# Three data movements of a hybrid decoder layer: gate stores moved to SyncE, a spilled operand loaded behind the value weights, raw value weights asked for earlier

## The chip, the cores and the metric

The kernel runs on one core of a Trainium2 chip. The metric is the device time of one execution in microseconds, the median of three runs. Five engines work side by side: TensorE (PE), VectorE (DVE), ScalarE (ACT), GpSimd (POOL) and SyncE (SP). ScalarE, GpSimd and SyncE also issue DMAs, each from its own instruction queue. An engine takes its instructions in order, so a DMA issue that has to wait for its data holds up everything behind it on that engine.

## The reference

One layer of a decoder trunk for a prompt of 2048 tokens and 8 single-token samples, 1024 wide, all in float32:

```
hn = rmsnorm(x, g_norm) * (1 + scale) + shift          # scale, shift, gate from silu(c) @ w_ada
z  = hn @ w_in                                          # xa, za (1024 each), q, k (512), v (1024), glr (16), zg (1024)
# RG-LRU: causal conv4 of xa, two block-diagonal gates, real-gated linear recurrence h, times silu(za)
# GLA, 4 heads (key 128, value 256): S_t = diag(alpha_t) S_{t-1} + k_t^T v_t, o_t = q_t S_t,
#   alpha from glr @ w_gla_g2; o = rmsnorm(o) * g_gla_norm * silu(zg)
x  = x + gate * (concat(y_lru, y_gla) @ w_out)
y  = rmsnorm(x, g_final)
```

The outputs are y for prompt and samples and the new convolution, recurrence and GLA states.

## The kernel before, in words

A float32 operand is split into a high part that TensorE multiplies in one pass and a low part, and a product is the sum of three passes: high times high, high times low, low times high. The three lines 661 to 663 (keys, queries, gates), 346 to 348 (values) and the loop of line 1566 are such triples.

The tokens are worked in two halves of 1024. `hn` of the half at work stands transposed in SBUF as `hh` (high) and `hl` (low), eight tiles of 128 features, 1024 columns and the samples. In each half the GLA heads follow in the order 3, 0, 1, 2 (`HEADS`), and between them stand the RG-LRU tiles. `gla_head` computes a head's values (`values`), then keys, queries and decay, and leaves the chunks of the recurrence to a list of due times (`after`, `tick`), so that they lie between later matrix products. In the second half, `values` also multiplies the samples by the raw, unsplit value weights (`sample_values`, line 912), which `raw_values` loads from `w_in` into the two buffers of the tag `wr` (line 333). Split weights lie in DRAM (`parts`) and are loaded by SyncE into the three buffers of the tag `w` (line 293).

Between the halves, `gates_ahead` computes gates of head 3 for the second tokens: six pieces of `silu2` (lines 1131 and 1132) that are stored in DRAM (`zgd`, line 1654) until the head's output needs them. In the same stretch `next_hn` modulates the next half of `hn`: TensorE transposes (line 197), ScalarE applies scale and shift (lines 199, 201), GpSimd rounds into `hh` (line 204) and VectorE forms `hl` (line 205). Behind it, seven-product schemes (`seven`, `product`, line 1566) compute further gates and RG-LRU inputs from sums of blocks of `hn`. One of these sums is put into the place of a block of `hn` itself, columns 512 to 1023 of the first four feature tiles (`a21`). That block is first spilled to DRAM (`a21d`, line 1524) and loaded back by `a21_back` (line 1532) for the values of head 3 in the second half, which read it from the fifth of their eight token tiles on.

Each engine's instruction order is settled when the program is compiled, by a scheduler with its own estimate of times: an instruction is placed when its inputs and its buffer are free in that estimate, in the order of the program where several are. Three helpers bend this order: `in_order` keeps the written order on each engine, `behind(q)` keeps what is written inside it behind the last instruction written for engine q, and `held(q)` makes the DMAs inside it wait until that last instruction has run.

Of the kernel before, what the change touches and what calls it, by code (L numbers as in the profile page):

```python
# [8 lines left out]
F32 = mybir.dt.float32  # L9
# [45 lines left out]
def hybrid_kernel(ctx, tc, i, o):  # L55
    nc = tc.nc
    V, S, G, PE, SP = nc.vector, nc.scalar, nc.gpsimd, nc.tensor, nc.sync
# [5 lines left out]
    def acc():  # L63
        return psum.tile([P, 512], F32, tag="acc", name="acc", bufs=4)
# [12 lines left out]
    zgd = dpool.tile([8, P, TH + NS], F32, tag="zgd", name="zgd")  # L77
    a21d = dpool.tile([2, P, 4, 512], F32, tag="a21d", name="a21d")
# [245 lines left out]
    def value_weights(h):  # L324
        n = DV + (RANK if h == HEADS[0] else 0)
        return [weights(V0 + h * DV, n, k0, 4) for k0 in (0, 4)]
# [12 lines left out]
    def drip():  # L339
        if drips:  # L340
            drips.pop(0)()
# [339 lines left out]
    def behind(q):  # L681

        return tc.issue_after(next(x for x in reversed(list(nc.cur_bb.bb.instructions)) if x.engine == q.engine))


    @contextmanager
    def held(q):

        traced = nc.cur_bb.bb.instructions
        mark = next(x for x in reversed(list(traced)) if x.engine == q.engine)  # L690
        before = {id(x) for x in traced}
        yield
        for x in list(traced):
            if id(x) not in before and x.engine in (SP.engine, G.engine):
                tc.add_manual_dep(x, mark.name, mybir.DependencyInfo(
                    mybir.DependencyClass.Sync, mybir.DependencyReason.DATA), reason="held")
# [4 lines left out]
    def after(units, fn, gla=False, val=False):  # L701
        clock[1] += 1
        heapq.heappush(pend, (clock[0] + units, clock[1], fn, gla, val))
# [221 lines left out]
    def new_values():  # L925
        while any(e[4] for e in pend):
            e = min(e for e in pend if e[3])
            pend.remove(e)
            heapq.heapify(pend)
            e[2]()  # L930
        return [[gp.tile([P, 4, DV], F32R, tag=tag, name=tag, bufs=2) for _ in range(2)] for tag in ("vh", "vl")]

    def values(half, h, w, back=None):
        first = h == HEADS[0]
        n = DV + (RANK if first else 0)
        vh, vl = new_values()
        turns = []
        for tt in range(8):
            if tt == 1 and back:
                with held(V):  # L940
                    back()
            if tt == 3 and half == 1:
                with held(V):
                    raw = raw_values(h, n)
            if tt == 4:
                while drips:
                    drip()
            if half == 0 or tt < 6:
                ps = acc()
                value_mm(ps[:, :n], slice(tt * P, (tt + 1) * P), w, n, (0, KT))  # L950
            elif tt == 6:
                both = [acc(), acc()]
                for k in (0, 4):
                    for m in range(2):
                        value_mm(both[m][:, :n], slice((6 + m) * P, (7 + m) * P), w, n, (k, k + 4))
                ps = both[0]
            else:
                ps = both[1]
            hi, lo = vh[tt // 4][:, tt % 4], vl[tt // 4][:, tt % 4]
            S.copy(hi, ps[:, :DV])  # L960
            V.tensor_tensor(lo, ps[:, :DV], hi.bitcast(F32), op=OP.subtract)  # L961
            if len(turns) == 3 or tt == 7 and turns:
                turns.pop(0)()
            if first:
                turns.append(low_rank(ps[:, DV:n], slice(0, P), tt * P))
            tick(0.5)
        if half == 1:
            turns.append(sample_values(h, raw, n))
        for f in turns:
            after(1, f, True)  # L970
        return vh, vl
# [201 lines left out]
    def gla_head(half, h, wv=None, ahead=None):  # L1173
        ns = len(SEGS[half])
        if wv:
            wk, wq = wkq0
            v, prep0, rest = first_head()
        else:
            w, back = value_weights(h), None
            if half and h == HEADS[0]:  # L1180
                back = a21_back
            v = values(half, h, w, back)
            wk = weights(K0 + h * DK, DK)
            wq = weights(Q0 + h * DK, DK)
        prep, zs, os_, state = {}, {}, [None], []

        def chunks(s, c):

            nch = min(SEGS[half][s][1], TH - SEGS[half][s][0]) // P
            if c == 0:  # L1190
                prep[s, "run"] = gla_start(half, h, s, prep[s])
                after(PACE[half][0], lambda: chunks(s, 1), True, True)
                return
            if c == nch and half:
                gate_load(s)
            gla_chunk(half, h, s, c - 1, prep[s], prep[s, "run"], v)
            if c < nch:
                after(PACE[half][1], lambda: chunks(s, c + 1), True, True)
                return
            gla_norm(nch, prep[s, "run"])  # L1200
            after(PACE[half][2] if half else 1 if s + 1 < ns else 2, lambda: finish(s), True)
            if s + 1 < ns:
                after(0, lambda: chunks(s + 1, 0), True, True)
            elif half == 1:
                G.dma_start(o[4][0, 0, h], St[h])

        def gate_load(s):
            c0, n = SEGS[half][s]
            for dt in range(2):
                z = new_zs()  # L1210
                G.dma_start(z[:, :n], zgd[2 * h + dt][:, c0:c0 + n])
                zs[s, dt] = z[:, :n]

        def finish(s):
            if (s, 1) not in zs or (s == 2 and os_[0] is None):
                after(0.5, lambda: finish(s), True)
                return
            gla_out(half, h, s, prep[s, "run"][1], os_[0] if s == 2 else None, [zs[s, 0], zs[s, 1]])

        def sample(smp, b0):  # L1220
            sample_state(h, smp, b0, state, lambda: os_.__setitem__(0, state[1]))

        pk = None
        if not wv:
            if h == HEADS[0]:

                pk = project(wk, *SEGS[half][0])
            dec = gla_decay(half, h, 0)
        for s in range(ns):
            if wv and s == 0:  # L1230
                prep[s] = prep0
                pk = project(wk, 512, 512)
                rest()
            else:
                prep[s] = gla_qk(half, h, s, wq, wk, dec, pk)
                pk = None
                if s == 0 and ahead:
                    with held(V):
                        ahead()
            if s + 1 < ns:  # L1240
                dec = gla_decay(half, h, s + 1)
            if s == 0:
                after(2 if h == HEADS[0] else 1, lambda: chunks(0, 0), True, True)
            tick()
        if half == 1:
            after(1, lambda: sample(prep[2][3], 0), True)
            after(3, lambda: sample(prep[2][3], 4), True)
        if wv:
            modulate_samples(st, xsr)
            hn_sample()  # L1250
            with tc.issue_after(last[V.engine]), tc.issue_after(last[S.engine]):
                constants()
            open_lp()
        if half == 1:
            return
        wz = [weights(ZG + (2 * h + dt) * P, P) for dt in range(2)]
        for s in range(ns):
            for dt in range(2):
                zs[s, dt] = gate_silu(wz[dt], s, 2 * h + dt)
                tick()  # L1260
# [225 lines left out]
    def a21():  # L1486
        return [(hh, hl)[u][:, :4, 512:TH] for u in range(2)]
# [39 lines left out]
        for n, u in ((0, 0), (1, 0), (0, 1), (1, 1), (2, 0), (2, 1), (3, 0), (3, 1), (4, 0), (4, 1)):  # L1527
            drips.append(lambda n=n, u=u: step(n, u))

    def a21_back():  # L1530
        for u, x in enumerate(a21()):
            G.dma_start(x.bitcast(F32), a21d[u])

    operands, lone, zq, zturn = [], [True], [], [0]

    def operand(src, shifted):
# [111 lines left out]
    def gates_ahead(h):  # L1648

        w = [weights(ZG + (2 * h + dt) * P, P) for dt in range(2)]  # L1650
        for c0, n in ((0, 256), (256, 256), (512, 512)):
            for dt in range(2):
                z = silu2(w[dt], c0, n)
                after(0.5, lambda z=z, dt=dt, c0=c0, n=n: S.dma_start(zgd[2 * h + dt][:, c0:c0 + n], z))
                tick(n / 512)
            if c0 == 256:
                while drips:
                    drip()
        sums()
# [521 lines left out]
    for n in range(2, 16):  # L2181
        g = n - 1
        x, prev = pairs[n], pairs[n - 1]
# [81 lines left out]
```

## Time and profile before

| | |
|---|---|
| Median of three runs | 1474.25 us (1472.72 to 1477.07) |
| Profiled execution | 1477.21 us, of which its span 1475.4 us |
| TensorE busy | 1435.1 us (97%) |
| VectorE, ScalarE, GpSimd busy | 1052.0, 688.7, 220.5 us |
| Mean granted TensorE clock | 0.988 |
| DMA traffic | 305.33 MB, 207 GB/s over the span |
| Spilled block of hn | two loads of 1024 KB from GpSimd, 6.7 and 8.3 us to landing |
| Raw value weights | eight loads of 512 to 544 KB from GpSimd, 4.8 to 8.1 us to landing |
| Gates stored by ScalarE in `gates_ahead` | four of 128 KB, two of 256 KB |

How to read the rows below: a row of a timeline has its start, its duration, the engine, the line of the kernel, the operation, what it writes and reads, and in brackets the engine's idle time just before it with what ended that. A row of waits has the total, the number and the longest. A row of a stretch has its bounds and length, then busy time and count for TensorE, its weight loads, VectorE, ScalarE and GpSimd, then the mean granted TensorE clock, the busy share of the DMA engines and GB/s. "SPq" and "ACTq" are instructions that only the engine's sequencer handles, such as DMA issues. Matmuls are pipelined, so a row of 0.29 us may follow another after 0.13 us.

### The profile page before, as it was taken

How to read it: one execution, taken by the hardware profiler on the slowest of the kernel's cores; microseconds unless marked ns; L12 is line 12 of the kernel's file. 1: busy time of each engine (PE TensorE's matmuls, PEld its weight loads, DVE VectorE, ACT ScalarE, POOL GpSimd, SP SyncE). 2: the span in 40 equal slices, each digit the busy share in tenths (PEclk: the TensorE clock that was granted, in tenths of full speed). 3: DMA queues.
4: the chain of work that ended last, by engine and by line, in shares of the span. 5: the costliest groups of instructions: out<-in, count | busy, mean ns of one | idle time of the engine just before them, and what ended most of it. 6: DMA issues, size and time to landing. Idle time of an engine off the chain costs nothing. (4 is left out here: it accounts for less than half of the span.)

```text
span 1475.4 us, 23576 instructions
## 1 busy us (share of the span) xinstructions
PE 1435.1 (97%) x8741; PEld 1262.3 (86%) x8741; DVE 1052.0 (71%) x2477; ACT 688.7 (47%) x1251; POOL 220.5 (15%) x366
## 2 busy tenths in 40 slices
PE   8999999999999999999999899998999999999998
PEld 6888989889898988788899899998998887778886
DVE  5757667776665769844468578585778986588886
ACT  4653544652544467534354354534557622144342
POOL 0200111222121112000212322323200000000000
PEclk9999999999999999999999999999999999999999
DMA  9655876866566454767646565656553757793453
GB/s 329 257 182 179 273 241 218 255 206 197 182 203 208 148 202 150 236 206 249 247 130 203 175 207 178 213 190 226 186 193 99 286 190 263 260 357 117 143 175 114
DMA packets 161241, 305.33 MB, mean 207 GB/s; under 512 B 12963, under 2 KB 91459, under 8 KB 158686
## 3 DMA queue, kind: packets, MB, share of 16 engines
q1 hardware_dynamic: 104917, 214.24, 42.6%
q0 software_dynamic: 23296, 72.54, 14.4%
q10 hardware_dynamic: 32912, 17.04, 3.8%
q8 instruction: 69, 1.13, 0.3%
q14 instruction: 47, 0.38, 0.1%
HBM read 188.51 MB, written 115.33 MB: 206 GB/s over the span
## 5 line engine op out<-in xcount | busy, mean ns | idle before, releaser
L661 PE MATMUL acc<-hh,w 128*128 128x512 f32 (+3 forms) x1112 | 388.8, 350 | 0.3 <-ACT tx L1319 0.2
L662 PE MATMUL acc<-hl,w 128*128 128x512 f32 (+3 forms) x1112 | 378.1, 340 | 0.0
L663 PE MATMUL acc<-hh,w 128*128 128x512 f32 (+3 forms) x1112 | 377.7, 340 | 0.0
L661 PEld LDWEIGHTS acc<-hh,w 128*128 128x128 f32 x1112 | 211.6, 190 | 17.5 <-ACT tx L1319 0.9
L662 PEld LDWEIGHTS acc<-hl,w 128*128 128x128 f32 x1112 | 211.4, 190 | 17.5 <-issue 1.2
L663 PEld LDWEIGHTS acc<-hh,w 128*128 128x128 f32 x1112 | 211.2, 190 | 16.3
L1851 PE MATMUL acc<-w,a 128*128 128x512 f32 (+1 forms) x792 | 184.8, 387 | 0.0
L1851 PEld LDWEIGHTS acc<-w,a 128*128 128x128 f32 x792 | 146.9, 188 | 33.1 <-issue 3.4
L346 PE MATMUL acc<-w,hh 128*128 128x256 f32 (+1 forms) x508 | 145.4, 286 | 2.5 <-DMA hh<-a21d 2.4
L348 PE MATMUL acc<-w,hl 128*128 128x256 f32 (+1 forms) x508 | 144.1, 285 | 0.9 <-DMA hl<-a21d 0.9
L347 PE MATMUL acc<-w,hh 128*128 128x256 f32 (+1 forms) x508 | 144.1, 284 | 0.0
L1851 PE MATMUL tp<-w,a 128*128 128x512 f32 x564 | 136.0, 391 | 0.0
L1851 PEld LDWEIGHTS tp<-w,a 128*128 128x128 f32 x564 | 105.3, 188 | 26.7 <-issue 5.1
L346 PEld LDWEIGHTS acc<-w,hh 128*128 128x128 f32 x508 | 97.0, 191 | 3.9 <-issue 2.7
L348 PEld LDWEIGHTS acc<-w,hl 128*128 128x128 f32 x508 | 97.1, 192 | 1.3 <-DMA hl<-a21d 1.3
L347 PEld LDWEIGHTS acc<-w,hh 128*128 128x128 f32 x508 | 97.0, 191 | 0.2
L1131 ACT ACTIVATE zs<-acc 128x512 f32<-128x512 f32 (+3 forms) x70 | 34.3, 491 | 104.1 <-PE acc L663 103.0
L1279 DVE SCALAR_TENSOR_TENSOR cv<-xa,vecT,cv 128x512 f32<-128x512 f32 (+2 forms) x120 | 76.4, 639 | 7.1 <-ACT cv L1277 6.7
L1701 ACT CAST a<-s 128x512 fp32r<-128x512 f32 x61 | 36.5, 619 | 96.1 <-issue 36.6
L1132 DVE SCALAR_TENSOR_TENSOR zs<-zs,acc 128x512 f32<-128x512 f32 (+3 forms) x70 | 38.5, 550 | 46.8 <-ACT zs L1131 46.7
L960 ACT CAST vh<-acc 128x256 fp32r<-128x256 f32 x56 | 20.4, 370 | 98.0 <-PE acc L348 82.8
L961 DVE TENSOR_TENSOR vl<-acc,vh 128x256 fp32r<-128x256 f32 x56 | 23.3, 421 | 53.3 <-ACT vh L960 53.3
(405 smaller groups left out, 2760.0 us busy)
## 6 DMA issues: line engine op xcount, KB each, us to landing
parts<-w SPq DMA_DIRECT2D x37, 1024.0 KB
w<-parts SPq DMA_DIRECT2D x28, 1024.0 KB
wr<-in_w_in_dram SPq DMA_DIRECT2D x38, 512.0 KB
a<-mixd SPq DMA_DIRECT2D x63, 256.0 KB
w<-wd SPq DMA_DIRECT2D x12, 1024.0 KB
w<-twd SPq DMA_DIRECT2D x20, 512.0 KB
mixd<-zs ACTq DMA_DIRECT2D x34, 256.0 KB
wada<-in_w_ada_dram SPq DMA_DIRECT2D x16, 512.0 KB
```

The lines of the kernel that those rows point to most:

```text
L346: PE.matmul(ps, hh[:, kt, c], hi[:, kt % 4], start=kt == 0, stop=False)
L347: PE.matmul(ps, hh[:, kt, c], lo[:, kt % 4], start=False, stop=False)
L348: PE.matmul(ps, hl[:, kt, c], hi[:, kt % 4], start=False, stop=kt == KT - 1)
L661: PE.matmul(ps[:, :n], hi[:, kt], a, start=kt == 0, stop=False)
L662: PE.matmul(ps[:, :n], hi[:, kt], b, start=False, stop=False)
L663: PE.matmul(ps[:, :n], lo[:, kt], a, start=False, stop=kt == KT - 1)
L961: V.tensor_tensor(lo, ps[:, :DV], hi.bitcast(F32), op=OP.subtract)
L1131: S.activation(z, ps, AF.Tanh, scale=0.5)
L1132: V.scalar_tensor_tensor(z, z, 1.0, ps, op0=OP.add, op1=OP.mult)
L1279: V.scalar_tensor_tensor(cv[:, cq], xa[:, cq.start + k:cq.stop + k], cw[k], cv[:, cq], op0=OP.mult, op1=OP.add)
L1701: S.copy(t[:, 0, k], (low(t) if src is None else src)[:, k])
L1851: PE.matmul(ps, t[:, u, k], w[:, v, k, c], start=(q < 3 or ps is own) and (k, u, v) == (0, 0, 0), stop=(k, u) == (3, 1), skip_group_check= ...
```

## The change

Three edits. The six stores of `gates_ahead` are issued by SyncE instead of ScalarE. The two loads of the spilled block are issued by SyncE, in program order right after the loads of the value weights and behind the last of them, instead of by GpSimd at the second value tile behind VectorE's mark. The raw value weights are asked for at the second token tile instead of the fourth for head 3, still behind VectorE's mark, and at the first token tile without a mark for the other heads.

```diff
-    def values(half, h, w, back=None):
+    def values(half, h, w):
...
         for tt in range(8):
-            if tt == 1 and back:
-                with held(V):
-                    back()
-            if tt == 3 and half == 1:
-                with held(V):
+            if half == 1 and tt == first:
+                with held(V) if first else ExitStack():
                     raw = raw_values(h, n)
...
-            w, back = value_weights(h), None
+            w = value_weights(h)
             if half and h == HEADS[0]:
-                back = a21_back
-            v = values(half, h, w, back)
+                with behind(SP):
+                    for u, x in enumerate(a21()):
+                        SP.dma_start(x.bitcast(F32), a21d[u])
+            v = values(half, h, w)
...
-    def a21_back():
-        for u, x in enumerate(a21()):
-            G.dma_start(x.bitcast(F32), a21d[u])
...
-                after(0.5, lambda z=z, dt=dt, c0=c0, n=n: S.dma_start(zgd[2 * h + dt][:, c0:c0 + n], z))
+                after(0.5, lambda z=z, dt=dt, c0=c0, n=n: SP.dma_start(zgd[2 * h + dt][:, c0:c0 + n], z))
```

## The prediction

> **What bounds the kernel now.** I read the page first, then the waits of TensorE, then a timeline of TensorE from which I kept only the rows with idle time, and last the other engines around those rows.
>
> ```profile
> span 1475.4 us, 23576 instructions
> ...
> PE 1435.1 (97%) x8741; PEld 1262.3 (86%) x8741; DVE 1052.0 (71%) x2477; ACT 688.7 (47%) x1251; POOL 220.5 (15%) x366
> ```
>
> ```profile
> PE acc L912 <- DMA wr<-in_w_in_dram: 9.7, 3, 4.8
> ```
>
> ```profile
> 586.20 0.33 PE L197 MATMUL tp<-ident,xst 128*128 128x128 f32 x1 [3.45 <-ACT fs L201]
> ...
> 613.53 0.50 PE L1566 MATMUL acc<-hh,w 128*128 128x512 f32 x1 [1.82 <-ACT acc L1580]
> ...
> 726.41 0.36 PE L346 MATMUL acc<-w,hh 128*128 128x272 f32 x1 [2.41 <-DMA hh<-a21d]
> ...
> 728.83 0.60 PE L348 MATMUL acc<-w,hl 128*128 128x272 f32 x1 [0.92 <-DMA hl<-a21d]
> ...
> 838.24 1.04 PE L912 MATMUL acc<-wr,fs 128*8 128x64 f32 x32 [4.44 <-DMA wr<-in_w_in_dram]
> ...
> 930.39 0.63 PE L912 MATMUL acc<-wr,fs 128*8 128x64 f32 x32 [0.53 <-DMA wr<-in_w_in_dram]
> ...
> 1026.04 1.04 PE L912 MATMUL acc<-wr,fs 128*8 128x64 f32 x32 [4.77 <-DMA wr<-in_w_in_dram]
> ...
> 1136.24 0.45 PE L1316 MATMUL acc<-xh,wg 128*128 128x384 f32 x1 [1.35 <-DVE zs L1132]
> ```
>
> TensorE is busy 97% of the span, so the kernel is bound by it, and a gain can only come out of the few places where it stands still. The bracket ends each row with the idle time and with what ended it. Six of these eight rows are what the change touches: the ScalarE wait at 586, the two loads of the spilled part of hn at 726 and 729, and the raw value weights at 838, 930 and 1026. Their idle time is 3.45 + 2.41 + 0.92 + 4.44 + 0.53 + 4.77 = 16.5 us.
>
> A gap costs more than its length, because the clock drops behind it. The columns after the stretch are its length, five pairs of busy time and count, then PEclk, the DMA share and GB/s.
>
> ```profile
> 586.20:592.00 5.80, 5.80 (x37) 5.80 (x38) 3.74 (x7) 2.53 (x6) 1.91 (x4) 0.71 0.06 23
> 613.00:623.00 10.00, 9.47 (x34) 7.67 (x35) 10.00 (x11) 4.89 (x7) 0.60 (x1) 0.83 0.81 261
> 728.00:734.00 6.00, 5.17 (x23) 5.17 (x24) 0.63 (x1) 0.00 (x0) 1.85 (x4) 0.50 0.87 318
> ...
> 1136.00:1146.00 10.00, 9.40 (x53) 8.87 (x54) 4.34 (x10) 7.95 (x11) 2.22 (x3) 1.00 0.62 225
> ...
> 720.00:728.00 8.00, 5.50 (x42) 4.81 (x40) 1.48 (x9) 0.74 (x2) 3.23 (x5) 0.97 0.97 373
> ```
>
> Behind the gaps of 3.45 us, 1.82 us and 2.41 + 0.92 us the granted clock is 0.71, 0.83 and 0.50; behind 1.35 us it stays 1.00. So in this trace a gap below about 1.4 us costs itself, and one above about 1.8 us costs work besides: (1 - 0.71) x 5.8 = 1.7 us at 586 and (1 - 0.83) x 10 = 1.7 us at 613. At 729, TensorE was busy 5.17 us at a clock of 0.50, which is 2.6 us of work lost; some of the 5.17 us is the pipelined end of a matmul, and I take 2.4.
>
> The Trainium skill (TensorE: Matmul & The Clock Gate, Part 1) lets the clock fall to half only after an idle window of about 3.4 us. The row of 0.83 behind a gap of 1.82 us disagrees, and the row decides. By that rule the sum below would lose the 2.4 us of the spilled part and give 1453.4 us.
>
> **Part 1, the first gates' stores move from ScalarE to SyncE.** Six stores leave ScalarE's queue.
>
> ```profile
> 584.66 0.34 ACTq L1654 DMA_DIRECT2D zgd<-zs  x1
> 585.12 0.56 ACT L199 ACTIVATE fs<-tp,Sh,Gm 128x256 f32<-128x256 f32 x1 [5.85 <-DVE zs L1132]
> ...
> 610.88 0.33 ACTq L1654 DMA_DIRECT2D zgd<-zs  x1
> ```
>
> ```profile
> 582.95 0.75 DVE L181 TENSOR_SCALAR xt<-xt,rs 128x1024 f32<-128x1024 f32 x1
> 583.61 0.68 DVE L205 TENSOR_TENSOR hl<-ra,hh 128x512 fp32r<-128x512 f32 x1
> 584.21 0.41 DVE L1132 SCALAR_TENSOR_TENSOR zs<-zs,acc 128x256 f32<-128x256 f32 x1
> ```
>
> The first store stands in ScalarE's queue until VectorE's L1132 has written the gates at 584.6. ScalarE is idle for 5.85 us ahead of L199, whose result frees the transposes' PSUM tiles for TensorE. With the store gone, ScalarE drains those tiles at once. What is late next is VectorE: the transposes that TensorE starts at 586.20 read the rows which L181 finishes only at 582.95 + 0.75 = 583.70. TensorE stopped at 586.20 - 3.45 = 582.75, so 0.95 us of the gap stay, which is below 1.4 us and keeps the clock. The gain is 3.45 - 0.95 + 1.7 = 4.2 us. VectorE runs almost without a pause from there to the next product (10.00 of 10.00 us in the stretch from 613 above), so it cannot follow all of that; I take off 1 us, and the part counts 3.2 us. Its bounds are 0 (VectorE holds everything) and 3.45 + 1.7 = 5.2 us. The six issues of 0.33 us that leave ScalarE, 2 us, are hidden: nothing behind them is late but what was counted.
>
> On SyncE the stores wait for the same L1132, and the loads of the next products' weights stand behind them.
>
> ```profile
> 606.30 1.17 SPq L1548 DMA_DIRECT2D w<-twd  x2
> 609.02 0.52 SPq L1548 DMA_DIRECT2D w<-parts  x1
> ```
>
> If the last store goes ahead of the load at 609.02, that load starts at about 611.2 instead, 2.2 us later. The product that runs when the load starts and the ones whose weights are there already cover it: the weights come into their slots three products ahead. A product takes about the 2.7 us that lie between the two issues above, each of which follows the end of one, so the cover is some 8 us against 2.2 us plus a load (0.5 MB, 1.4 us at the 373 GB/s of the fullest stretch). I cost it at nothing; without that cover it would be 2.2 us and, at more than 1.8 us, the clock's 1.7 us too. The gap of 1.82 us at 613 has another cause (ScalarE's own stores into mixd stay) and remains.
>
> **Part 2, the spilled part of hn.** Two loads of 1 MB move from GpSimd, held until VectorE reached a mark, to SyncE behind the value weights.
>
> ```profile
> 719.58 0.75 POOL L1532 DMA_DIRECT2D hh<-a21d  x1 [1.25 <-issue]
> 720.51 0.75 POOL L1532 DMA_DIRECT2D hl<-a21d  x1 [0.18 <-issue]
> ```
>
> ```profile
> hl<-a21d POOLq DMA_DIRECT2D x1, 1024.0 KB, 8.3
> ```
>
> ```profile
> 706.16 0.32 SPq L293 DMA_DIRECT2D w<-parts  x1
> ```
>
> ```profile
> 712.92 0.29 PE L346 MATMUL acc<-w,hh 128*128 128x272 f32 x1
> ...
> 723.51 0.49 PE L896 MATMUL tp<-ident,g 128*48 128x128 f32 x3
> ```
>
> The value tiles read the loaded columns from the fifth one on, behind the transposes at 723.51. SyncE has issued the second half of the value weights at 706.16 and is then free. The loads' place in hh and hl was read last by a product that ends before the values begin, so even the latest start, about 712, lands by 712 + 8.3 = 720.3, ahead of 723.51. The whole of 2.41 + 0.92 + 2.4 = 5.7 us goes. Behind the loads on SyncE stands the key weights' load, which waits for a weight slot anyway. GpSimd is rid of two issues of 0.75 us, and its raw loads follow sooner. The bounds are 0 and 5.7 us.
>
> **Part 3, the raw value weights.** For the first head the loads are asked for two value tiles earlier, with the hold; that head has no wait on them, so it counts 0. For the other three they are traced three tiles earlier and without a hold.
>
> ```profile
> 826.19 0.76 POOL L333 DMA_DIRECT2D wr<-in_w_in_dram  x1 [0.18 <-issue]
> ...
> 830.48 0.77 POOL L333 DMA_DIRECT2D wr<-in_w_in_dram  x1
> ```
>
> ```profile
> L912 PE MATMUL acc<-wr,fs x64: 218/250/315, 833.2 to 839.0; 128*8 128x64 f32 x64
> ...
> L976 PE MATMUL acc<-gls,g2s x2: 340/515/690, 839.2 to 849.8; 128*128 128x384 f32 x2
> ...
> L912 PE MATMUL acc<-wr,fs x64: 218/219/223, 929.2 to 930.8; 128*8 128x64 f32 x64
> ...
> L976 PE MATMUL acc<-gls,g2s x2: 340/392/443, 931.0 to 939.7; 128*128 128x384 f32 x2
> ...
> L912 PE MATMUL acc<-wr,fs x64: 218/248/315, 1020.6 to 1026.8; 128*8 128x64 f32 x64
> ...
> L976 PE MATMUL acc<-gls,g2s x2: 340/514/689, 1027.0 to 1037.6; 128*128 128x384 f32 x2
> ```
>
> The second load of the head at 833 is issued at 830.48 and landed at 838.24, 7.8 us later. The rows of part 2 put 84 matmuls of 272 columns between 712.92 and 723.51, 0.126 us each, so 0.119 us for 256 columns, and three value tiles of 24 matmuls take some 8.5 us. So even with the same queue ahead of it the load starts at about 822 and lands at 830, ahead of its reader at 833.8. The price is read from the three heads themselves, from the first L912 to the second L976: 849.8 - 833.2 = 16.6 us, 939.7 - 929.2 = 10.5 us and 1037.6 - 1020.6 = 17.0 us. The middle head, which waited only 0.53 us, shows what the same work takes undisturbed, and that nothing else (key and query weights, decay) becomes late when TensorE arrives early. The gain is 6.1 + 6.5 us, and 0.53 us for each of the three: 14.2 us. The bounds are 0 and 14.2 us.
>
> **The sum** is 3.2 + 5.7 + 14.2 = 23.1 us. The profiled execution took 1477.21 us, 1.8 us more than its span, and the median of the three runs is 1474.25; a saving on TensorE's own line comes off each alike, and 1474.25 - 23.1 = 1451.2 us. I give 1451.
>
> **The rivals.** About 0.3% (4.4 us) is what a measurement of this kernel can tell from no change.
>
> *The raw loads stay late in GpSimd's queue.* Its queue waits for VectorE and for other DMAs, and the second of the pair trails the first by 830.48 - 826.19 = 4.3 us. If the queue's waits and not the program's order place the loads, half of part 3 is lost, 7.1 us: 1458 us. Against it: nothing that GpSimd does for an earlier head needs these loads to be late. Chance 0.10.
>
> *The spilled part collides with the value weights.* The second half of the weights, a little over 1 MB issued at 706.16, is read at 712.92. Two more MB behind it share the same engines; at the 373 GB/s of the fullest stretch all 3.2 MB take 8.6 us, to 714.8, and 8.3 us for the second of two 1 MB loads leave 2.7 us beyond their 2.1 MB at that rate. So the wait would be 714.8 + 2.7 - 712.9 = 4.6 us, with 1.7 us of clock 6.3 us. That undoes part 2: 1457.5 us. For the forecast speaks that the weights stand ahead on the same queue. The Trainium skill (DMA: Bandwidth & Descriptors, Issuing engines are not separate DMA queues) says that transfers of all issuing engines interleave on the same 16 engines; no run here shows it yet. Chance 0.08.
>
> *Slower: the raw loads take the wrong head's buffers.* The tag wr has two buffers. Without the hold, the second head's loads are ready as soon as both are free, while the first head's still wait for their mark. If the schedule hands a buffer to whoever is ready first, the first head's samples wait for the second head's, a head's length later (929.2 - 833.2 = 96 us), and everything behind its sample rows (its last gates, then the second head's outputs) with them. It decides from the moment that the first head's mark falls behind the freeing of the buffers. I estimate 25 to 50 us of TensorE idle, of a delay of 96 us that other work partly fills, against 9 us gained: 1490 to 1515 us. Against it:
>
> ```profile
> 1021.38 6.13 SPq L1966 DMA_DIRECT2D wr<-mixd  x2
> ```
>
> These loads, of mixed rows of the first half of the tokens, which was done before the gates at 584, use the same two buffers and did not take them while they stood free between heads; they came when the last head had let go. Chance 0.07.
>
> *No change:* new waits of VectorE and SyncE take the place of the old ones, as after any new order of four queues. 1470 to 1478 us, chance 0.05.
>
> **How the numbers follow.** The forecast itself, 1445 to 1456, has 0.66; the first two rivals 0.18; 0.04 is left for a loss of two parts at once (1459 to 1469); no change 0.05, slower 0.07. The range from 1445 to 1464 takes in the forecast's upper bound (parts at 5.2 + 5.7 + 14.2 = 25.1 us, and some 4 us of scatter) and the first two rivals. Faster by over 0.3%: 0.66 + 0.18 + 0.04 = 0.88; within 0.05; slower 0.07.
>
> **What would show it.** Right: no row of L912 waits for wr, L346 and L348 do not wait for a21d, L197 waits under 1.4 us and for VectorE, and the clock near 590, 730, 840 and 1028 (moved up by what was saved before) is 1.00. The six L1654 issues stand on SPq and the a21d loads within 2 us behind the value weights. Wrong: a wait on w ahead of L346 at the first values, L912 rows out of order or still waiting, or L1566 waiting for w near 615.

## The result and the profile after

The changed kernel takes 1455.43 us (median of four executions, 1454.42 to 1459.8), beside 1475.66 us for the kernel before (1472.72 to 1477.33): a ratio of 0.9871 with a 95% interval of 0.9843 to 0.9898. The profiled execution took 1454.69 us. Forecast were 1451 us, with a range of 1445 to 1464. So the gain is 20.2 us by medians and 22.5 us by the two profiled spans, against a forecast of 23.1 us.

From the page of the changed kernel, then from its waits of TensorE:

```profile
span 1452.9 us, 23584 instructions
...
PE 1424.1 (98%) x8741; PEld 1250.8 (86%) x8741; DVE 1051.5 (72%) x2477; ACT 689.6 (47%) x1251; POOL 220.0 (15%) x364
```

```profile
PE acc L1561 <- DVE so L1497: 1.5, 2, 1.2
...
PE tp L197 <- DVE xst L181: 1.2, 1, 1.2
...
PE acc L1561 <- DVE ra L1497: 0.8, 1, 0.8
```

No DMA of the three edits is left in that list: no row of L912 waits for `wr`, none of L346 or L348 for `a21d`. TensorE's busy time fell by 11 us although it does the same 8741 matmuls, because the half-speed stretches of the clock between 587 and 1031 us are gone. (The lines are numbered anew: L1561 is the L1566 of before, L1649 its L1654, L1072 its L1075, L1846 its L1851.) The idle rows of TensorE in the stretch of the gates, and the stretches behind the places where the clock was 0.71, 0.50 and below 1 before:

```profile
583.35 0.30 PE L197 MATMUL tp<-ident,xst 128*128 128x128 f32 x1 [1.22 <-DVE xst L181]
...
617.44 1.67 PE L1561 MATMUL acc<-so,w 128*128 128x512 f32 x6 [1.20 <-DVE so L1497]
...
620.85 0.50 PE L1561 MATMUL acc<-ra,w 128*128 128x512 f32 x1 [0.81 <-DVE ra L1497]
...
794.43 0.38 PE L1072 MATMUL po<-vh,amh 128*128 128x256 f32 x1 [0.52 <-DVE on L1081]
```

```profile
583.35:590.00 6.65, 6.28 (x50) 5.89 (x51) 5.51 (x11) 2.32 (x5) 0.80 (x2) 1.00 0.13 42
...
728.00:734.00 6.00, 6.00 (x103) 5.67 (x103) 2.03 (x10) 0.74 (x2) 0.22 (x1) 1.00 0.52 181
822.00:832.00 10.00, 10.00 (x124) 9.76 (x123) 4.66 (x15) 5.71 (x11) 3.60 (x6) 1.00 0.85 282
1005.00:1015.00 10.00, 9.77 (x114) 9.24 (x114) 6.06 (x17) 6.35 (x12) 2.64 (x6) 1.00 0.68 232
```

The wait of 3.45 us for ScalarE at 586 is now 1.22 us for VectorE, and the next one, 1.82 us for ScalarE near 613, has become waits for VectorE at 617 and 621. SyncE's timeline shows the moved stores and loads, GpSimd's the raw loads:

```profile
584.82 4.74 SPq L1649 DMA_DIRECT2D zgd<-zs  x3
...
608.74 0.33 SPq L1649 DMA_DIRECT2D zgd<-zs  x1
609.16 0.53 SPq L1543 DMA_DIRECT2D w<-parts  x1
...
702.61 0.32 SPq L293 DMA_DIRECT2D w<-parts  x1
703.02 0.53 SPq L1180 DMA_DIRECT2D hh<-a21d  x1
703.61 1.06 SPq L1180 DMA_DIRECT2D hl<-a21d  x1
```

```profile
733.78 0.76 POOL L333 DMA_DIRECT2D wr<-in_w_in_dram  x1 [7.01 <-PE acc L912]
...
736.57 0.78 POOL L333 DMA_DIRECT2D wr<-in_w_in_dram  x1
```

The spilled part follows the value weights directly. The raw weights of head 0 are issued at 733.78, as soon as head 3's samples (L912) have let go of the buffers, 91 us ahead of their reader at 824.45. That was not forecast, and it matters below.

To see where the time came from, I cut the span at the same instructions in each profile: the transposes near 575, the first L346 of head 3's values, the first L912 of each head, the first matmul of the final stage (L1851, now L1846), the end. Lengths in us; "again" is the profiled execution of the same changed kernel in e4, e9 a version that comes later.

| from, to | before | after | again (e4) | e9 |
|---|---|---|---|---|
| transposes, values of head 3 (part 1) | 136.31 | 133.37 | 133.35 | 133.35 |
| values, samples of head 3 (part 2) | 31.25 | 24.83 | 24.83 | 24.83 |
| samples of head 3, of head 0 | 90.51 | 91.77 | 91.70 | 90.88 |
| head 0, head 1 | 96.07 | 89.80 | 92.81 | 89.05 |
| head 1, head 2 | 91.41 | 90.90 | 90.91 | 90.92 |
| head 2, final stage | 130.13 | 123.25 | 127.33 | 123.26 |
| final stage, end | 324.67 | 324.51 | 324.54 | 324.54 |

Part 1 gave 2.9 us, part 2 6.4 us, part 3 (the four rows of heads) 408.1 - 395.7 = 12.4 us. Of the rest, 0.6 us lie ahead of the transposes, where nothing was changed, and 0.2 us in the final stage. In the other execution part 3 gave only 408.1 - 402.7 = 5.4 us.

### The profile page after: what moved, and what is told of

The parts are those of the page before. It is cut to its first block, busy times and chain, and to the rows that moved or that the text cites. A ratio compares the mean times of both kernels' runs of the same rounds, so it can differ in the third digit from the quotient of the medians.

```text
span 1452.9 us, 23584 instructions
## 1 busy us (share of the span) xinstructions
PE 1424.1 (98%) x8741; PEld 1250.8 (86%) x8741; DVE 1051.5 (72%) x2477; ACT 689.6 (47%) x1251; POOL 220.0 (15%) x364
## 5 line engine op out<-in xcount | busy, mean ns | idle before, releaser
L661 PE MATMUL acc<-hh,w 128*128 128x512 f32 (+3 forms) x1112 | 386.1, 347 | 0.5 <-DVE xb L999 0.2
L661 PEld LDWEIGHTS acc<-hh,w 128*128 128x128 f32 x1112 | 209.2, 188 | 18.1 <-ACT tx L1318 0.9
L663 PEld LDWEIGHTS acc<-hh,w 128*128 128x128 f32 x1112 | 209.1, 188 | 16.3
L1846 PE MATMUL acc<-w,a 128*128 128x512 f32 (+1 forms) x792 | 184.8, 386 | 0.0
L1846 PEld LDWEIGHTS acc<-w,a 128*128 128x128 f32 x792 | 146.8, 188 | 33.2 <-issue 3.4
L346 PE MATMUL acc<-w,hh 128*128 128x256 f32 (+1 forms) x508 | 144.7, 285 | 0.0
L348 PE MATMUL acc<-w,hl 128*128 128x256 f32 (+1 forms) x508 | 143.5, 282 | 0.2 <-DVE hl L228 0.2
L1846 PE MATMUL tp<-w,a 128*128 128x512 f32 x564 | 136.0, 391 | 0.0
L1846 PEld LDWEIGHTS tp<-w,a 128*128 128x128 f32 x564 | 105.2, 188 | 26.8 <-issue 5.2
L346 PEld LDWEIGHTS acc<-w,hh 128*128 128x128 f32 x508 | 95.5, 188 | 1.3 <-ACT zs L1128 0.4
L348 PEld LDWEIGHTS acc<-w,hl 128*128 128x128 f32 x508 | 96.2, 189 | 0.4 <-DVE hl L228 0.4
```

Of the source, the lines that this page charges most:

```text
L346: PE.matmul(ps, hh[:, kt, c], hi[:, kt % 4], start=kt == 0, stop=False)
L348: PE.matmul(ps, hl[:, kt, c], hi[:, kt % 4], start=False, stop=kt == KT - 1)
L661: PE.matmul(ps[:, :n], hi[:, kt], a, start=kt == 0, stop=False)
L663: PE.matmul(ps[:, :n], lo[:, kt], a, start=False, stop=kt == KT - 1)
L1846: PE.matmul(ps, t[:, u, k], w[:, v, k, c], start=(q < 3 or ps is own) and (k, u, v) == (0, 0, 0), stop=(k, u) == (3, 1), skip_group_check= ...
```

## The experiments

**Each part alone (e1 to e4).** e1 is the kernel before with this edit alone, e2 with the move of the spilled part alone, e3 with the earlier raw loads alone, all as in the diff of the change; e4 is the changed kernel again.

```diff
-                after(0.5, lambda z=z, dt=dt, c0=c0, n=n: S.dma_start(zgd[2 * h + dt][:, c0:c0 + n], z))
+                after(0.5, lambda z=z, dt=dt, c0=c0, n=n: SP.dma_start(zgd[2 * h + dt][:, c0:c0 + n], z))
```

> The kernel before with only the six gate stores moved from ScalarE's queue to SyncE's. Theory (the parts are independent, and each brings what its own stretch of the trace lost): about 3 us less, ratio 0.998; in the profile the wait of L197 falls from 3.45 us to below 1.5 us and is ended by VectorE, the granted clock behind it is 1.00 and not 0.71, and the wait of 1.82 us for ScalarE near 613 turns into waits for VectorE. The spilled part (2.41 + 0.92 us) and the raw weights (4.44 + 0.53 + 4.77 us) are waited for as before. Rival (the saving is swallowed by the next late thing, since the loads of hn and of the raw weights are not moved and TensorE only comes to them sooner): ratio 1.000, with the waits for a21d and wr longer by the 3 us.

> The kernel before with only the two loads of the spilled part moved to SyncE behind the value weights. Theory: 5.7 to 6.4 us less, ratio 0.996; no wait for a21d at L346 and L348, granted clock 1.00 in the stretch behind them, L197 still waits 3.45 us and L912 still for the raw weights. Rival (the loads collide with the value weights): L346 waits for w near 711 for some 4.6 us, ratio 1.000.

> The kernel before with only the raw value weights asked for at their head's beginning. Theory: 14 us less, ratio 0.990; no row of L912 waits for wr, and the granted clock behind each is 1.00. The waits for a21d (2.41 + 0.92 us) and of L197 (3.45 us) stay. Rival (GpSimd's queue is fuller here than in the changed kernel, since the loads of the spilled part are still in it with their hold): the first head's raw loads are still late or push those of the spilled part back, 1.5 to 7 us of the gain are missing, ratio 0.992 to 0.995.

> The changed kernel again, beside its three parts on the same chip. Theory (additive): the savings of the three runs sum to its saving within 2 us, 20 to 23 us, ratio 0.985 to 0.987. Rival (the parts share a resource): the sum of the three differs from it by 4 us or more.

| run | median us | ratio to before, 95% | gain by the ratio, us |
|---|---|---|---|
| e1, stores alone | 1474.82 | 0.9997 (0.9986 to 1.0007) | 0.4 |
| e2, spilled part alone | 1471.78 | 0.9973 (0.9959 to 0.9987) | 4.0 |
| e3, raw weights alone | 1463.99 | 0.993 (0.9916 to 0.9944) | 10.3 |
| e4, all three | 1456.29 | 0.9869 (0.9853 to 0.9885) | 19.3 |

By the ratios the parts alone sum to 0.4 + 4.0 + 10.3 = 14.7 us, against 19.3 us together; by the medians alone it is 16.2 us. The intervals leave each gain open by 1.5 to 2.4 us, so the times show a loss only just beyond the noise. That e1 falls short of the 3 us expected is clear: its interval reaches from -1.0 to 2.1 us. The waits of TensorE in e1, then idle rows of e2 and of e3, one execution of each:

```profile
PE acc L912 <- DMA wr<-in_w_in_dram: 11.2, 3, 5.9
PE acc L346 <- DMA hh<-a21d: 4.3, 1, 4.3
```

```profile
830.83 0.35 PE L912 MATMUL acc<-wr,fs 128*8 128x64 f32 x12 [1.31 <-DMA wr<-in_w_in_dram]
...
1017.45 1.04 PE L912 MATMUL acc<-wr,fs 128*8 128x64 f32 x32 [6.42 <-DMA wr<-in_w_in_dram]
```

```profile
728.36 0.56 PE L346 MATMUL acc<-w,hh 128*128 128x272 f32 x1 [5.19 <-DMA hh<-a21d]
...
1022.46 0.66 PE L661 MATMUL acc<-hh,w 128*128 128x384 f32 x1 [2.79 <-DMA w<-parts]
```

In e1 the stretch of part 1 is 133.35 us long, the same 2.96 us shorter as in the changed kernel. TensorE then comes earlier to loads that were not moved: it waits 4.3 us instead of 2.4 for `hh`, and 11.2 us instead of 9.7 for the raw weights. At the spilled part this costs nothing: the stretch takes 31.30 us, against 31.25 before, because the wait for `hl` is shorter and the clock stays at half for 3.41 us instead of 6.83. The four stretches of heads take 409.6 us instead of 408.1, so about half of the 3.0 us is left in this profile. The rival of e1's expectation holds in this part: a gain ahead of a load that does not come earlier is swallowed there.

e2 keeps the whole of part 2 (24.82 us). Its profile is the fastest of its nine executions and does not show why the median gained only 4.0 us: the last head's wait grew from 4.77 to 6.42 us, but the first one's fell from 4.44 to 1.31 us. In e3 nothing ahead of the spilled part was moved. Its two loads are issued at 719.77 and 720.70, as late as before, the wait for `hh` is 5.19 us instead of 2.41 + 0.92, and the stretch is 0.9 us longer. L912 never waits, but at 1022.46 TensorE waits 2.79 us for the query weights, and the clock falls to half behind it; the stretch from head 2 to the final stage is 4.3 us longer than in the changed kernel's first profile. This is the slowest of e3's six executions. The same wait comes back in e4, so this edit alone is enough for it.

e4 showed something else. Its profiled execution has a span of 1460.5 us, 7.6 us more than the first profile of the same kernel, and two new waits. The rows are TensorE's, then SyncE's:

```profile
832.43 0.41 PE L661 MATMUL acc<-hh,w 128*128 128x384 f32 x1 [1.89 <-DMA w<-parts]
...
1016.41 0.41 PE L661 MATMUL acc<-hh,w 128*128 128x384 f32 x1 [2.18 <-DMA w<-parts]
```

```profile
822.16 0.52 SPq L293 DMA_DIRECT2D w<-parts  x1
...
1005.89 0.52 SPq L293 DMA_DIRECT2D w<-parts  x1
1009.31 1.11 SPq L1961 DMA_DIRECT2D wr<-mixd  x2
```

These rows of L661 wait for the query weights, 1 MB. Those of the first row are issued at 822.16, when the value weights' place is free, and wanted at 832.43 - 1.89 = 830.54, 8.4 us later. Two half-speed stretches of the clock (below) cost 1.7 us each: 1.89 + 2.18 + 3.4 = 7.5 us. The two stretches of heads that hold them are 7.1 us longer than in the first profile, and 0.5 us of the difference lies ahead of the transposes, so these two waits are what makes this execution slower. Before, TensorE stood still in front of the same place for the raw weights, and the query weights were never last.

**Raw loads behind the mark (e5, e6).** e5 is the changed kernel with the hold for all heads, e6 with the loads two tiles later in the other three heads.

```diff
             if half == 1 and tt == first:
-                with held(V) if first else ExitStack():
+                with held(V):                                  # e5
...
-            if half == 1 and tt == first:
-                with held(V) if first else ExitStack():
+            if half == 1 and tt == (1 if first else 2):        # e6
+                with held(V):
```

> The changed kernel, with the raw loads of the other three heads asked for at the same place but held behind VectorE's mark, as the first head's are: they can no longer be issued right behind the head before, some 90 us ahead. Theory A (the prediction's: an issue 8 us ahead of the reader is enough, and the key weights are late in some executions because the next head's raw loads, issued at 825.9 and 828.9, share the DMA engines with them): no row of L912 waits for wr, no row of L661 waits for w, 1452 to 1455 us with little scatter, ratio 0.985. Rival B (only an issue far ahead is safe, since GpSimd's queue is filled by other waits during the values): L912 waits again in one head or two, 1.5 to 5 us each and as much again in clock, 1459 to 1466 us. Rival C (the key weights are late for another reason): no wait for wr, but L661 waits for w by 2 us in one or two heads as in the changed kernel, 1454 to 1462 us.

> As the run before, but the raw loads of the other heads are asked for two value tiles later (third tile instead of the first; in the kernel before it was the fourth). Theory A (what counts is the time from issue to landing, 4 to 8 us, against a distance that shrinks by some 2.9 us for each value tile): waits for wr come back in one or two heads, shorter than the 4.44 and 4.77 us of before, in sum 1 to 6 us; 1457 to 1464 us. Where a gap is below 1.4 us the granted clock behind it stays 1.00, where it is over 1.8 us it falls. Rival B (the queue's waits place the loads, not the program's order): the waits are those of before, 9.7 us in three heads, 1468 us.

e5: 1456.18 us (1454.3 to 1456.76), ratio 0.9866 (0.9844 to 0.9888). e6: 1471.69 us, ratio 0.9974 (0.996 to 0.9989). GpSimd's row of e5, then GpSimd's and TensorE's of e6:

```profile
816.85 1.51 POOL L333 DMA_DIRECT2D wr<-in_w_in_dram  x2
```

```profile
820.92 0.78 POOL L333 DMA_DIRECT2D wr<-in_w_in_dram  x1
...
1007.99 1.52 POOL L333 DMA_DIRECT2D wr<-in_w_in_dram  x2
```

```profile
828.79 0.63 PE L912 MATMUL acc<-wr,fs 128*8 128x64 f32 x32 [4.08 <-DMA wr<-in_w_in_dram]
...
1015.58 1.04 PE L912 MATMUL acc<-wr,fs 128*8 128x64 f32 x32 [4.94 <-DMA wr<-in_w_in_dram]
...
1017.71 1.04 PE L912 MATMUL acc<-wr,fs 128*8 128x64 f32 x32 [1.08 <-DMA wr<-in_w_in_dram]
```

In e5 the loads of head 0 are issued 825.52 - 816.85 = 8.7 us ahead of their reader, and nothing waits for them (their landing takes 5.4 to 7.5 us). So some 8.5 us are enough, as theory A had it, with about a microsecond to spare. The time of e5 is higher than A's 1452 to 1455 us, and no row of L661 waits for `w` in its profile, as A had it; one profile is little to show that. In e6 the waits are 4.08 + 4.94 + 1.08 us, as much as before, not the 1 to 6 us of theory A. Two value tiles are 5.7 us of matmuls by the prediction's rate, but the distance from the issue to TensorE's arrival at the samples did not shrink by that much everywhere. In the last head it fell from 1006.2 - 996.5 = 9.7 us in e5 to 1010.6 - 1008.0 = 2.6 us in e6 (1010.6 is 1015.58 - 4.94), so by 7.1 us; for the two loads of head 0 it fell by 1.0 and by 4.8 us. Other issues of GpSimd (L857, L864, L829, L1210) now stand ahead of the last head's loads and between the two of head 0. Both theories hold a part: the program's place decides, but through what the compiled queue then puts ahead.

**The spilled part by another engine, or ahead of the weights (e7, e8).**

```diff
-                with behind(SP):
-                    for u, x in enumerate(a21()):
-                        SP.dma_start(x.bitcast(F32), a21d[u])
+                for u, x in enumerate(a21()):                  # e7
+                    G.dma_start(x.bitcast(F32), a21d[u])
...
-            w = value_weights(h)                               # e8, head 3 only
+                w = [weights(V0 + h * DV, DV + RANK, 0, 4)]
...                                                             # the two loads of a21d
+                    w.append(weights(V0 + h * DV, DV + RANK, 4, 4))
```

> The changed kernel, with the two loads of the spilled part issued by GpSimd at the same place of the program and without a hold, and not by SyncE behind the value weights. Theory (only the time of the issue counts, not the engine): they are issued before 713, L346 and L348 do not wait for a21d, and the time is that of the changed kernel, 1453 to 1460 us. Rival (GpSimd's queue is the cause: an issue that waits for the last reader of hh and hl stands ahead of the stores of gates and the raw loads): L346 waits again, 1 to 3 us and clock, or the last product waits for GpSimd's loads, 1458 to 1465 us.

> The changed kernel, with the two loads of the spilled part put ahead of the second half of the value weights on SyncE instead of behind it. Theory (the order on one queue decides, and the 2 MB take some 6 us ahead of it): L346 waits for w at the first value tile, 3 to 6 us and 1.7 us or more of clock, 1458 to 1463 us. Rival (the transfers share the engines evenly whatever the order, or the loads are early enough): no wait on w above 0.5 us, 1454 to 1458 us.

e7: 1455.94 us (1455.01 to 1457.03), ratio 0.9868 (0.9846 to 0.9891). e8: 1457.69 us (1457.16 to 1458.67), ratio 0.9881 (0.9858 to 0.9903). GpSimd's rows of e7, TensorE's of e8, and SyncE's issue of the second half of the value weights in e8:

```profile
705.41 0.77 POOL L1179 DMA_DIRECT2D hh<-a21d  x1 [0.70 <-issue]
707.80 0.76 POOL L1179 DMA_DIRECT2D hl<-a21d  x1
```

```profile
716.91 0.39 PE L346 MATMUL acc<-w,hh 128*128 128x272 f32 x1 [1.35 <-DMA w<-parts]
```

```profile
705.13 0.68 SPq L293 DMA_DIRECT2D w<-parts  x1
```

With GpSimd issuing at 705 and 708 the stretch from values to samples is 24.83 us, exactly that of the changed kernel. The engine does not matter; what cost 6.4 us was the later issue, at 719.58 and 720.51. With the loads ahead of the weights' second half TensorE waits for the weights, 1.35 us, and the stretch is 26.67 us. That is the collision of the prediction's second rival, in the reverse order, with a wait of 1.35 us where 3 to 6 were expected. The load itself is late by as much as was expected, and the compiled order hides most of it. In e8 48 matmuls, the first halves of four tiles, stand ahead of the second half's first reader, and the half is there 716.91 - 705.13 = 11.8 us after its issue. In the changed kernel, where a tile is done at once, its thirteenth matmul reads that half without a wait at 709.36, 6.8 us after the issue at 702.61. So the 2 MB ahead cost this load 5 us or more. For the changed order the collision did not come.

**Room for the query weights (e9, e10).** e9 holds the raw loads as e5 does and puts two loads of mixed rows, which take the `wr` buffers behind the last head's samples, behind SyncE's later loads. e10 does only the latter.

```diff
-        SP.dma_start(r, mixd[2 * x.p + 1, :, CTS[0]:CTS[0] + 8].rearrange("p (q k) t -> p q k t", q=2))
+        with behind(SP):
+            SP.dma_start(r, mixd[2 * x.p + 1, :, CTS[0]:CTS[0] + 8].rearrange("p (q k) t -> p q k t", q=2))
```

> The changed kernel with two loads taken out of the stretch in which the query weights (1 MB, issued when the last value matmul has freed their place, read some 8.4 us later) are on their way: the raw loads of the other heads held at their own head's beginning, as in e5, and the two loads of mixed rows that take the wr buffers behind the last head's samples put behind SyncE's later loads (about 1071 instead of 1006). Theory (the query weights are late in some executions because 1 MB of other loads is issued within the same 8 us): no row of L661 waits for w in any head; 1452 to 1455.5 us, and less scatter than the 1454.0 to 1462.4 of the changed kernel. Rival (the wait has another source, such as the gates' or the state's transfers): L661 still waits by 2 us in one head or more in the profiled run or the times still reach 1458 us. Second rival (the later mixed rows are now missed at the beginning of the final stage): a wait for wr or a near 1080 to 1130, some us.

> The changed kernel with only the loads of mixed rows put later; the raw loads are still issued right behind the head before, beside the query weights. Theory of e9: the last head's wait (2.18 us at 1016 in e4) can no longer come, the first ones (1.89 us at 832) still can: 1453 to 1458 us, between the changed kernel and e9. Rival: no difference from the changed kernel in scatter and median.

e9: 1453.56 us (1452.69 to 1454.77), ratio 0.9854 (0.9838 to 0.987), span 1451.8 us. e10: 1455.33 us (1453.8 to 1459.75), ratio 0.9872 (0.9853 to 0.9891). SyncE's and GpSimd's rows of e9 beside the query weights, and TensorE's of e10:

```profile
821.38 0.53 SPq L293 DMA_DIRECT2D w<-parts  x1
```

```profile
815.33 1.51 POOL L333 DMA_DIRECT2D wr<-in_w_in_dram  x2
```

```profile
830.73 0.41 PE L661 MATMUL acc<-hh,w 128*128 128x384 f32 x1 [0.48 <-DMA w<-parts]
```

With nothing of these loads issued in the 8 us of the query weights, no L661 waits, and the five times lie within 2.1 us, against 8.3 us for the nine executions of the changed kernel (median 1456.18 us, 1454.04 to 1462.35). e10, where the raw loads still go beside the query weights, keeps a wait of 0.48 us at the same place and a scatter of 6 us. Over all profiles L661 waits for `w` only where one of these loads is issued in that window (e3, e4, e10, and 0.59 us in e11; 0.83 us at the same place in e7 are put down to VectorE), but not always: the first profile of the changed kernel and e8 have both loads there and e5 the mixed rows, without such a wait, and e7 and e8 scatter by 2.0 and 1.5 us only. So the shared window makes the wait possible; what decides in which execution it comes stays open, and that every slower execution has it was not seen, since each run leaves one profile. e9 is the fastest version, 2.6 us below the changed kernel by these medians, though the intervals of the two ratios overlap.

**The stores by GpSimd (e11).**

```diff
-                after(0.5, lambda z=z, dt=dt, c0=c0, n=n: SP.dma_start(zgd[2 * h + dt][:, c0:c0 + n], z))
+                after(0.5, lambda z=z, dt=dt, c0=c0, n=n: G.dma_start(zgd[2 * h + dt][:, c0:c0 + n], z))
```

> The changed kernel with the six gate stores in GpSimd's queue instead of SyncE's. Theory (what matters is that ScalarE is rid of them, but an issue that waits for data blocks what is behind it on whatever engine has it; SyncE has nothing urgent behind, GpSimd has its parts of the next split and the low-rank stores): L197 no longer waits for ScalarE, but a wait for GpSimd's work appears between 584 and 640, 1 to 4 us; ratio 0.987 to 0.990. Rival (any engine but ScalarE does): the same time as the changed kernel, 1454 to 1457 us, and no new wait above 0.5 us.

e11: 1457.26 us (1453.66 to 1457.91), ratio 0.9874 (0.9855 to 0.9892). TensorE's row, then GpSimd's queue ahead of it:

```profile
589.98 0.42 PE L197 MATMUL tp<-ident,xst 128*128 128x128 f32 x1 [2.44 <-DVE ra L203]
```

```profile
587.49 0.59 POOL L1649 DMA_DIRECT2D zgd<-zs  x1 [1.35 <-ACT zs L1128]
588.12 0.63 POOL L204 TENSOR_SCALAR hh<-fs 128x512 fp32r<-128x512 f32 x1
```

The store waits for the gates, GpSimd's split (L204) waits behind the store, VectorE waits for the split, and TensorE for VectorE. Part 1's stretch is 135.50 us, so 2.1 of its 2.9 us are lost again. By time alone e11 cannot be told from the changed kernel; its stretch and its rows decide for the theory.

## Why the prediction was right, and where it was off

**What bounds the kernel.** Right: the gain came out of the six waits and the clock behind them, and nothing of the final stage moved (324.67 and 324.51 us).

**Part 1, 3.2 us forecast.** 2.9 us measured. The residue at L197 is 1.22 us, for VectorE, where 0.95 was worked out, and the clock is kept. That the gap of 1.82 us at 613 "has another cause" and remains failed: it went, with its half-speed window, and new waits for VectorE of 1.20 and 0.81 us at 617 and 621 took its place. Compared matmul by matmul from the transposes on, TensorE's lead over the kernel before is 3.3 us at 591, 2.5 us ahead of that gap's place, 6.1 us behind it and 3.0 us at 625. So VectorE's pace sets the end of this part; it took back 3.1 us where 1 us was set aside, out of a gain that was not forecast, and that 2.9 and 3.2 us agree so well is partly luck. The loads behind the stores on SyncE, costed at nothing, were never waited for. What the step did not say is that it depends on the others: alone it brought 0.4 us (e1, at most 2.1 by its interval).

**Part 2, 5.7 us forecast.** 6.4 us measured: besides the waits of 2.41 and 0.92 us, the half-speed stretch there cost 3.1 us rather than 2.4.

**Part 3, 14.2 us forecast.** Right in mechanism: L912 never waits, and e5 shows that the 8.5 us of the working are enough. Wrong in placement. The loads were not issued at about 822 but at 733.78, 825.43 and 915.44, right behind the head before, because without a hold the schedule issues them as soon as the two buffers are free. The prediction used that rule for its third rival, the wrong head's buffers, but not for its own sum. The cost is the mis-sized term: the middle head was read as showing "that nothing else (key and query weights, decay) becomes late when TensorE arrives early". The query weights can become late, when another megabyte is issued in their 8 us. So part 3 gave 12.4 us in one profile and 5.4 in another, where 14.2 was forecast. With the loads kept out of those 8 us (e9) it gave 408.1 - 394.1 = 14.0 us. The query weights are therefore part of what lies between the forecast of 1451 us and the measured 1455.43, but not all: e9 still takes 1453.56 us. Another 1.4 us come from the kernel before, whose median was 1475.66 us in this comparison and 1474.25 us when the forecast was made. A rest is open: from head 3's samples to head 0's the changed kernel is 1.3 us slower than before, of which 0.52 us is the wait at 794.43, and e9 0.4 us slower.

**The rivals.** The spilled part did not collide (no L346 waits for `w`; e8 shows the collision in the other order). The Trainium skill's sentence on transfers of all issuing engines interleaving (DMA: Bandwidth & Descriptors, Issuing engines are not separate DMA queues) fits what the runs show in a place that the prediction had not looked at: GpSimd's raw loads and SyncE's query weights. No head took another's buffers.

## What to carry to other kernels

A wait removed from the bounding engine is kept only up to the next load whose time does not depend on that engine; cost a chain of edits as a chain, and do not be surprised if one of them alone measures as nothing. A load that is issued as early as its buffer allows is not free: it can land on a transfer that is then short of time, so look at what is under way in that window, and hold the early load to the latest time that is still safe. A DMA issue that waits for data belongs in the queue of an engine that has nothing urgent behind it.

## What the runs showed of the hardware

The clock falls in windows of a fixed grid. The half-speed stretches of the kernel before from 580 to 1100 us begin at 587.54, 614.85, 727.49, 836.71 and 1024.45, and each lasts 3.41 or 6.83 us; the distances are 8, 33, 32 and 55 times 3.413 us. Stretches of the kernel before, of e3, of e9 and of e6, cut at the grid of each execution (e3's from its own half-speed stretch at 585.23, e9's from one at 23.91, e6's from one at 1013.62):

```profile
611.44:614.85 3.41, 1.59 (x8) 1.10 (x7) 3.41 (x5) 1.94 (x3) 0.00 (x0) 1.00 0.99 280
614.85:618.26 3.41, 3.41 (x10) 2.67 (x9) 3.41 (x4) 0.08 (x1) 0.00 (x0) 0.50 0.88 295
```

```profile
609.12:612.54 3.42, 1.99 (x9) 1.31 (x7) 3.42 (x6) 0.14 (x1) 0.00 (x0) 1.00 0.99 325
612.54:615.95 3.41, 2.60 (x11) 2.17 (x12) 3.41 (x4) 2.02 (x3) 0.00 (x0) 1.00 1.02 349
615.95:619.36 3.41, 3.41 (x16) 2.79 (x16) 3.41 (x4) 0.66 (x1) 0.00 (x0) 1.00 0.69 218
```

```profile
1109.35:1112.76 3.41, 1.77 (x14) 1.45 (x13) 3.41 (x10) 1.08 (x3) 0.00 (x0) 1.00 0.24 71
1112.76:1116.17 3.41, 3.07 (x16) 2.53 (x17) 2.78 (x8) 1.47 (x4) 1.75 (x3) 1.00 0.58 217
```

```profile
1013.62:1017.03 3.41, 1.04 (x32) 0.79 (x32) 0.00 (x0) 0.00 (x0) 0.00 (x0) 0.50 1.00 398
1017.03:1020.45 3.42, 2.74 (x38) 2.54 (x39) 0.65 (x2) 1.00 (x3) 0.52 (x1) 0.50 0.74 222
1020.45:1023.86 3.41, 3.41 (x12) 3.41 (x12) 1.61 (x5) 3.34 (x5) 1.51 (x3) 0.50 0.39 136
```

Before, the gap of 1.82 us lay inside one window, which was busy 1.59 of 3.41 us, and the next window ran at 0.50. In e3 a longer gap at the same place, 2.24 us, fell on both sides of a grid line (1.43 and 0.81 us idle) and cost no clock. In e9 a gap of 1.64 us lay inside one window, which was busy 1.77 us, and the next kept 1.00. So what counts is how much of one window is idle: 1.82 of 3.41 us was enough, 1.64 was not, and the limit lies near half. All thirteen profiles agree, from 20 us to 11 us before the end: each of the 24 windows at full clock that a half-speed one followed was busy for 1.60 us or less, and each of the others for 1.74 us or more. The prediction's bounds of 1.4 and 1.8 us fit only gaps that lie inside one window. The Trainium skill (TensorE: Matmul & The Clock Gate, Part 1) describes a free-running window of 3413 ns, and the grid agrees; its condition of an idle window does not, since half an idle window sufficed. The clock stays down for another window when the half-speed one is itself not full: in e6 windows busy for 1.04 and 2.74 us were followed by half speed, one busy for 3.41 us by full speed. Over all profiles the border lies near 2.7 us (2.72 us in e3 at 585.23 ended it).
